# Modulation sums on GpSimd instead of VectorE and TensorE, and a lower load rate in the feed forward

## The chip, the cores and the metric

The program runs on one core of a Trainium2 chip. The metric is device time in microseconds from one launch, as the median of several runs. The engines are called as the profile calls them: TensorE (PE), its weight load (PEld), VectorE (DVE), ScalarE (ACT), GpSimd (POOL) and SyncE (SP), which here only issues loads.

## The reference

Two transformer-like blocks on a sequence of 256 tokens with 2048 features, in float32. In both, a conditioning vector `c` of 2048 numbers gives six modulation vectors of 2048 numbers each:

```python
c_act = jax.nn.silu(c)
mod = c_act @ w_ada[l] + b_ada[l]          # w_ada: 2048 x 12288
sh1, sc1, g1, sh2, sc2, g2 = split(mod, 6)
h = rms_norm(x, norm_mix_g) * (1.0 + sc1) + sh1
x = x + g1 * mixer(h)
h2 = rms_norm(x, norm_mlp_g) * (1.0 + sc2) + sh2
x = x + g2 * (square(relu(h2 @ w_ff1)) @ w_ff2)
```

The first block's mixer is a state-space branch and an attention branch with gates (`w_in`, `w_glu`, `w_proj_ssm`, `w_proj_attn`, `w_out`); its feed forward has 8192 hidden features. The second block has another mixer (`w_in_2`, `w_out_2`) and, in place of the feed forward, a lookup of expert rows by index (`peer_down`, `peer_up`). The twelve modulation vectors are read here by the pair (block, number): (1, 1) and (1, 0) are the first block's `sc1` and `sh1`, (2, 5) is the last gate of the second block.

## The kernel before

**Weight gemms.** A weight matrix is read in pieces of four k-chunks by 512 columns, 1 MB each (`piece`). A piece is split by ScalarE into a rounded half (`wh`, 1.9 us) and by VectorE into the rest (`wl`, a two-operand subtraction over 128x2048), and TensorE multiplies both by the two halves of the activations (`gemm`, tiles `ga` and `gb`). A piece costs 48 matmuls of 256 columns or 24 of 512. The halves have two buffers each (tags "H" and "L").

**Modulation vectors.** One vector is a product of `c_act` with 16 tiles of 128x2048 of the modulation weights, 1 MB each (`aw`). There are two ways: `ada_pe` lets TensorE multiply each tile by a replicated column of `c_act` (tile `adap`); `ada` calls `ada_acc`, where VectorE multiplies each tile by a column and adds it into a sum over partitions (`acc`, or `gB` for the vector (2, 5)), and at the end TensorE sums over the partitions with one set of four matmuls (`ada`), followed by a copy and transposes (`ada_fin`, tile `adat`). The vectors (1, 1) and (1, 0) are always made by `ada_pe`, ahead of everything else. The string `TUNE["pe"]` names the numbers of the first block's further vectors that go by `ada_pe`: "24" before, so (1, 2) and (1, 4).

**What sets the order.** Both kinds of loads are issued by SyncE and take their buffers from one ring of four (pool `wp`, tag "W"). The vectors wait in one list, `stream`. Inside `gemm`, after every group of matmuls, `bg` adds a credit, and for each whole credit one step of the first vector in the list is taken, that is one `aw` tile. The credit per piece is `rate`: `TUNE["r1"]`, 0.65 up to `w_out`; `TUNE["r2"]` in the feed forward, 0.84 before; 0.5 in `w_in_2`. The number that a step yields is VectorE time, counted against the credit for other VectorE work (`work`: state-space steps, attention heads). `need` takes all the steps that are left of the vectors it names, at once; it stands ahead of `w_out`, in the feed forward after its second block, and ahead of the feed forward's last gemm, where the five vectors (2, 1), (2, 0), (2, 2), (2, 4) and (2, 3) must be there:

```python
        while cred[1] >= 1.0 and stream:
            cred[1] -= 1.0
            cred[0] -= step(stream, False)
...
            if end:
                need((2, 1), (2, 0), *[(2, s_[1]) for s_ in later[:TUNE["nf"]]])
```

In most of the program a scheduler then arranges the instructions of each engine; in a few stretches (`pinned`) the order is that of the code. GpSimd's instructions are never pinned except the late gathers. GpSimd issues small loads at the start, then nothing, and from about 2000 us the gathers of expert rows (`gather`, tiles `dn` and `up`), whose dot products VectorE makes (`dn` with `htok`, a two-operand instruction).

Of the kernel before, what the change touches and what calls it, by code (L numbers as in the profile page):

```python
# [15 lines left out]
OP = mybir.AluOpType  # L16
# [15 lines left out]
def _consts():  # L32
# [29 lines left out]
    for j in range(512):  # L62
# [9 lines left out]

NU = 14

TUNE = {"r1": 0.65, "d1": 3.6, "pe": "24", "r2": 0.84, "d2": 3.0, "rg": 0.5, "dq": 5.2, "dk": 4.0, "dr": 2.6, "dx": 3.9,
        "do": 5.0, "ro": 0.0, "nf": 3, "tail": 2}


# [1 line left out]
def tile_kernel(ctx: ExitStack, tc: tile.TileContext, I, out):  # L80
# [20 lines left out]
    V, S, T = Pinned(nc.vector), Pinned(nc.scalar), Pinned(nc.tensor)  # L101
    G, SY = nc.gpsimd, nc.sync
    uid = [0]

    def nm(s):
        uid[0] += 1
        return f"{s}_{uid[0]}"
# [8 lines left out]
    dr = ctx.enter_context(tc.tile_pool(name="dr", bufs=1, space=DRAM))  # L116
# [4 lines left out]
    def unit(shape, name="u", dt=F32):  # L121
        return up.tile(shape, dt, name=nm(name), tag="U")
# [9 lines left out]
    def pacc_(shape, name="a"):  # L132
        return psa.tile(shape, F32, name=nm(name), tag="A")

    def pmisc(shape, name="m"):
        return psb.tile(shape, F32, name=nm(name), tag="B")
# [69 lines left out]
    def start(g, first=False):  # L206
        if first:
            work.insert(0, g)
        else:
            work.append(g)  # L210
        return g
# [5 lines left out]
    ccol = {1: cT[:, 0:16], 2: cT[:, 16:32]}  # L217
    mods = {}

    def ada_acc(blk, j, acc):  # L220
        w = adaw[blk]
        for kc in range(NC):
            wt = wp.tile([P, D], F32, name=nm("aw"), tag="W")
            SY.dma_start(wt, w[kc * P:(kc + 1) * P, j * D:(j + 1) * D])
            if kc == 0:
                V.tensor_scalar(acc, wt, ccol[blk][:, 0:1], None, op0=OP.mult)
            else:
                V.scalar_tensor_tensor(acc, wt, ccol[blk][:, kc:kc + 1], acc, op0=OP.mult, op1=OP.add)
            yield 2.2

    def ada_fin(blk, j, ps, dest, g):
        ev = scr([P, 512], "adae")
# [12 lines left out]
    def ada(blk, j, g=None):  # L245

        dest = const([P, 16], "mod")
        acc = unit([P, D], "acc")
        yield from ada_acc(blk, j, acc)
        ps = pmisc([P, 512], "ada")  # L250
        for q in range(4):
            T.matmul(ps[32 * q:32 * q + 32, :], ones[:, 0:32], acc[:, 512 * q:512 * q + 512],
                     start=True, stop=True, skip_group_check=True)
        ada_fin(blk, j, ps, dest, g)
        yield 0.2
# [77 lines left out]
    def rsqrt_of(ps, scale, w, r1=None):  # L333

        al = tiny if w <= 32 else scr
        v = al([P, w], "rv")
        if r1 is not None:
            V.tensor_mul(v, r1, r1)
            V.tensor_mul(v, v, ps)
            ps = v  # L340
        V.tensor_scalar(v, ps, scale, EPS, op0=OP.mult, op1=OP.add)
        r = al([P, w], "rr")
        S.activation(r, v, AF.Sqrt)
        V.reciprocal(r, r)
        t = al([P, w], "rt")
        V.tensor_mul(t, v, r)
        V.scalar_tensor_tensor(t, t, -0.5, r, op0=OP.mult, op1=OP.mult)
        V.scalar_tensor_tensor(r, t, 1.5, r, op0=OP.add, op1=OP.mult)
        return r
# [121 lines left out]
    def total(st):  # L471
        r = tiny([P, 2], "tot")
        V.tensor_reduce(r, st, axis=AX.X, op=OP.add)
        return r
# [448 lines left out]
    def queue_ada(*specs, pe=False):  # L923
        def run():
            for b_, j_, *g_ in specs:
                g_ = g_[0] if g_ else None
                yield from (ada_pe(b_, j_, g_, crep) if pe else ada(b_, j_, g_))
        stream.append(run())
# [6 lines left out]
    for j, g_ in ((2, None), (4, "norm_mlp_g"), (3, None), (5, None)):  # L935
        queue_ada((1, j, g_), pe=str(j) in TUNE["pe"])

    def store_pairs(dst, base, func=AF.Copy, scale=1.0):
        def ev(i, b):
            c = base + 2 * i  # L940
            S.activation(dst[c // 8][:, c % 8:c % 8 + 2, :], b, func, scale=scale)
        return ev

    uT = unit([P, 8, L], "uT")
    for nb in range(2):
        gemm(w_in, NC, nb * 512, [("A", 512, store_pairs([uT], 4 * nb))], h, rate=TUNE["r1"], dve=TUNE["d1"], pre=pre if nb == 0 else ())

# [48 lines left out]
    def moba(h0, h1):  # L996
        for hd in range(h0, h1, 2):
            pts = yield from attn_probs([(qT[:, hd + j, :], kT[:, hd + j, :]) for j in range(2)],
                                        [bias[:, hd + j, :] for j in range(2)])
            o = pmisc([P, 2, L], "o")  # L1000
            for j in range(2):
                hs = slice((hd + j) * P, (hd + j + 1) * P)
                attn_pv(o[:, j, :], pts[j], vt[:, 0, hs], vt[:, 1, hs], True, True)
            V.tensor_copy(qT[:, hd:hd + 2, :], o)
            yield 0.7
# [4 lines left out]
    for nb in range(2):  # L1010
        gemm(w_in, NC, 1024 + nb * 512, [("A", 512, store_pairs([qT], 4 * nb, scale=SCALE))], h, rate=TUNE["r1"], dve=TUNE["d1"])
    for nb in range(2):
        gemm(w_in, NC, 2048 + nb * 512, [("A", 512, store_pairs([kT], 4 * nb))], h, rate=TUNE["r1"], dve=TUNE["d1"])
    vt = unit([P, 2, 1024], "vt")
    g_moba = []
    for nb in range(2):
        def ev_v(i, b, nb=nb):
            S.copy(vt[:, i, nb * 512:nb * 512 + 512], b)
        gemm(w_in, NC, 3072 + nb * 512, [("B", 512, ev_v)], h, rate=TUNE["r1"], dve=TUNE["d1"])
        g_moba.append(start(moba(4 * nb, 4 * nb + 4), first=True))  # L1020

    sgb = [unit([P, 8, L], "sgb") for _ in range(2)]
    for nb in range(4):
        gemm(w_in, NC, 6144 + nb * 512, [("A", 512, store_pairs(sgb, 4 * nb, AF.Tanh, 0.5))], h, rate=TUNE["r1"], dve=TUNE["d1"])
        if nb == 2:
# [130 lines left out]
    r2 = rsqrt_of(total(sq2), 1.0 / D, 2, r1c)  # L1156
# [18 lines left out]
    def gt2_bcast():  # L1175
        acc = unit([P, D], "gB")
        yield from ada_acc(2, 5, acc)
        br = wp.tile([1, D], F32, name=nm("gb"), tag="W")
        SY.dma_start(br, I["ada_b_2"][:, 5 * D:6 * D])
        for q in range(4):  # L1180
            sl = slice(512 * q, 512 * q + 512)
            ps = pmisc([P, 512], "gbp")
            T.matmul(ps, ones, acc[:, sl], start=True, stop=False)
            T.matmul(ps, ones[0:1, :], br[:, sl], start=False, stop=True)
            S.copy(acc[:, sl], ps)
            yield 0.0
        mods["gB"] = acc
# [551 lines left out]
    for i in range(16):  # L1739
        qt, hd, ei, g, dots = items[i]  # L1740
        if hd == 0:
            acc = [pacc_([P, 512], "pe") for _ in range(3)] + [pmisc([P, 512], "pe")]
# [80 lines left out]
```

## Time and profile before

| | |
|---|---|
| median of 3 runs | 3320.3 us (3318.84 to 3320.39) |
| the profiled execution's own time | 3320.44 us |
| its span, first to last instruction | 3318.7 us, 39085 instructions |
| mean granted TensorE clock | 0.975 of 2.4 GHz |
| TensorE busy | 2966.0 us (89%) |
| VectorE busy | 2268.4 us (68%) |
| ScalarE busy | 951.7 us (29%) |
| GpSimd busy | 817.5 us (25%) |

Stages, by the first and last matmuls on their activations: the two first vectors and the normed input up to 114 us; projections, attention, state space and `w_out` from there to 806 us; feed forward to 1550 us; `w_in_2` from 1560 to 1853 us; then `w_out_2` and the expert rows to the end. Busy times of engines overlap; the share over the whole span is a mean of stages with different limits, so what one stage is bound by is read from that stage.

### The profile page before, as it was taken

How to read it: one execution, taken by the hardware profiler on the slowest of the kernel's cores; microseconds unless marked ns; L12 is line 12 of the kernel's file. 1: busy time of each engine (PE TensorE's matmuls, PEld its weight loads, DVE VectorE, ACT ScalarE, POOL GpSimd, SP SyncE). 2: the span in 40 equal slices, each digit the busy share in tenths (PEclk: the TensorE clock that was granted, in tenths of full speed). 3: DMA queues.
4: the chain of work that ended last, by engine and by line, in shares of the span. 5: the costliest groups of instructions: out<-in, count | busy, mean ns of one | idle time of the engine just before them, and what ended most of it. 6: DMA issues, size and time to landing. Idle time of an engine off the chain costs nothing.

```text
span 3318.7 us, 39085 instructions
## 1 busy us (share of the span) xinstructions
PE 2966.0 (89%) x15580; PEld 2151.7 (65%) x15580; DVE 2268.4 (68%) x3360; ACT 951.7 (29%) x1271; POOL 817.5 (25%) x540
## 2 busy tenths in 40 slices
PE   6899999999999999999999998988877768777777
PEld 2687889998998889997999886444322223222222
DVE  7687689877788888877766647545655565555642
ACT  1323433444443343345336731111111101111000
POOL 1000000000000000000000005556666666666663
PEclk8899999999999999999999998999999989999999
DMA  9866667877899999984883448999999999999998
GB/s 367 303 224 212 208 228 239 300 273 241 285 328 336 328 335 328 328 288 155 280 273 115 153 165 358 419 418 420 421 422 421 422 422 421 422 421 421 422 421 340
DMA packets 280459, 1068.90 MB, mean 322 GB/s; under 512 B 27380, under 2 KB 35991, under 8 KB 189525
## 3 DMA queue, kind: packets, MB, share of 16 engines
q1 hardware_dynamic: 202306, 524.35, 45.8%
q0 software_dynamic: 74752, 538.26, 39.1%
q10 hardware_dynamic: 3220, 3.81, 0.4%
q8 instruction: 122, 2.00, 0.2%
q14 instruction: 59, 0.48, 0.0%
HBM read 1064.24 MB, written 2.11 MB: 321 GB/s over the span
## 4 chain that ended last, share of the span: by engine, by line
PE 61%; DMA 29%; DVE 5%; issue 2%; POOL 1%; ACT 1%; SPq 0%; POOLq 0%; ACTq 0%; DVEq 0%
PE ga L94 31%; DMA dn<-in_peer_down_dram,eid 24%; PE gb L94 18%; PE pe L94 4%; DMA up<-in_peer_up_dram,eid 3%; DVE dn L94 2%; PE adap L94 2%; DMA aw<-in_w_ada_dram 2%; PE xt L94 1%; PE bu L94 1%; PE yp L94 1%; PE wqp L94 1%; PE o L94 1%; DMA up<-in_peer_up_dram,er 1%; POOL dn L1689 1%
## 5 line engine op out<-in xcount | busy, mean ns | idle before, releaser
L94 PE MATMUL pe<-up,cdg 128*128 128x512 f32 x1792 | 831.7, 613 | 258.9 <-DMA up<-in_peer_up_dram,eid 189.4
L1689 POOL DMA_INDIRECT dn<-in_peer_down_dram,eid x256 | 499.4, 1951 | 2256.4 <-DVE g L94 1969.3
L94 DVE SCALAR_TENSOR_TENSOR dn<-dn,htok 128x2048 f32<-128x2048 f32 x256 | 586.0, 2291 | 482.5 <-DMA dn<-in_peer_down_dram,eid 482.4
L94 PEld LDWEIGHTS pe<-up,cdg 128*128 128x128 f32 x1792 | 336.5, 195 | 744.0 <-issue 510.7
L94 ACT ACTIVATE wh<-w 128x2048 fp32r<-128x2048 f32 (+1 forms) x284 | 538.9, 1897 | 876.3 <-PE ga L94 488.5
L94 DVE TENSOR_TENSOR wl<-w,wh 128x2048 fp32r<-128x2048 f32 (+1 forms) x284 | 643.1, 2265 | 193.0 <-ACT wh L94 144.2
L1689 POOL DMA_INDIRECT up<-in_peer_up_dram,eid x224 | 266.5, 1190 | 155.6 <-issue 51.5
L94 DVE SCALAR_TENSOR_TENSOR acc<-aw,cT,acc 128x2048 f32<-128x2048 f32 x105 | 246.6, 2348 | 48.1 <-DMA aw<-in_ada_w_dram 29.9
L94 PE MATMUL ga<-h2h,wh 128*128 128x256 f32 x1024 | 249.1, 283 | 0.0
L94 PE MATMUL ga<-h2l,wh 128*128 128x256 f32 x1024 | 248.6, 283 | 0.0
L94 PE MATMUL ga<-h1h,wh 128*128 128x256 f32 x896 | 224.1, 289 | 0.0
L94 PE MATMUL ga<-h1l,wh 128*128 128x256 f32 x896 | 220.4, 284 | 0.0
L94 PE MATMUL gb<-wh,ah 128*128 128x512 f32 x512 | 199.6, 390 | 0.0
L94 PE MATMUL gb<-wh,al 128*128 128x512 f32 x512 | 199.4, 390 | 0.0
L94 PEld LDWEIGHTS ga<-h2h,wh 128*128 128x128 f32 x1024 | 196.5, 192 | 1.9 <-issue 1.7
L94 PEld LDWEIGHTS ga<-h2l,wh 128*128 128x128 f32 x1024 | 196.5, 192 | 0.2
L94 PEld LDWEIGHTS ga<-h1h,wh 128*128 128x128 f32 x896 | 172.7, 193 | 19.5 <-issue 15.3
L94 ACT ACTIVATE cdg<-ca,cf 128x128 f32<-128x128 f32 x224 | 77.0, 393 | 356.4 <-PE pe L94 345.9
L94 PEld LDWEIGHTS ga<-h1l,wh 128*128 128x128 f32 x896 | 172.9, 193 | 0.9 <-issue 0.8
L94 PE MATMUL ga<-h2h,wl 128*128 128x256 f32 x1024 | 134.1, 283 | 0.0
L94 PE MATMUL ga<-h3l,wh 128*128 128x256 f32 x528 | 132.1, 288 | 0.0
L94 PE MATMUL ga<-h3h,wh 128*128 128x256 f32 x528 | 132.0, 288 | 0.0
(444 smaller groups left out, 4327.4 us busy)
## 6 DMA issues: line engine op xcount, KB each, us to landing
w<-in_w_ff_dram SPq DMA_DIRECT2D x128, 1024.0 KB, 6.6
w<-in_w_in_dram SPq DMA_DIRECT2D x100, 1024.0 KB, 5.6
aw<-in_w_ada_dram SPq DMA_DIRECT2D x96, 1024.0 KB, 7.2
aw<-in_ada_w_dram SPq DMA_DIRECT2D x96, 1024.0 KB, 6.3
w<-in_w_out_dram SPq DMA_DIRECT2D x32, 1024.0 KB, 5.1
wq<-in_peer_wq_dram SPq DMA_DIRECT2D x16, 1024.0 KB, 10.2
w<-in_w_proj_attn_dram SPq DMA_DIRECT2D x8, 1024.0 KB, 5.0
w<-in_w_proj_ssm_dram SPq DMA_DIRECT2D x8, 1024.0 KB, 5.7
```

The source lines that it names most:

```text
L94: r = f(*a, **k)
L1689: r = G.indirect_dma_start(out=rows_, out_offset=None, in_=table, in_offset=bass.IndirectOffsetOnAxis(ap=idx, axis=0))
```

## The change

All vectors that were made by VectorE, and the two that TensorE made besides the first two, now go through `ada_acc`, and `ada_acc` issues on GpSimd. GpSimd has two instructions in place of VectorE's one: a multiply in place, then an add into the sum. The steps no longer count VectorE time, and the feed forward's rate of tiles per piece is 0.66.

```diff
-TUNE = {"r1": 0.65, "d1": 3.6, "pe": "24", "r2": 0.84, "d2": 3.0, ...
+TUNE = {"r1": 0.65, "d1": 3.6, "pe": "", "r2": 0.66, "d2": 3.0, ...
...
             if kc == 0:
-                V.tensor_scalar(acc, wt, ccol[blk][:, 0:1], None, op0=OP.mult)
+                G.tensor_scalar(acc, wt, ccol[blk][:, 0:1], None, op0=OP.mult)
             else:
-                V.scalar_tensor_tensor(acc, wt, ccol[blk][:, kc:kc + 1], acc, op0=OP.mult, op1=OP.add)
-            yield 2.2
+                G.tensor_scalar(wt, wt, ccol[blk][:, kc:kc + 1], None, op0=OP.mult)
+                G.tensor_add(acc, acc, wt)
+            yield 0.0
```

The change moves instructions on every engine. GpSimd, beside the first projections: before, the gathers of expert rows (`dn`) stand directly behind the two small copies of the attention bias.

```order
28 L855 DMA rdr<-rrs_343 8x512
29 L858 DMA rev_346<-rdr 128x8x256
30 L1689 DMA dn_18006<-in_peer_down_dram,eid_17995 128x2048
31 L1689 DMA dn_18011<-in_peer_down_dram,eid_17995 128x2048
32 L1689 DMA dn_18016<-in_peer_down_dram,eid_17995 128x2048
```

Now the tiles of vector (1, 2) stand there (the number is the tile's):

```order
28 L856 DMA rdr<-rrs_343 8x512
29 L859 DMA rev_346<-rdr 128x8x256
30 L226 ISA
31 L226 TENSOR_SCALAR acc_1123<-aw_1124,cT_94 128x2048
32 L228 TENSOR_SCALAR aw_1211<-aw_1211,cT_94 128x2048
33 L228 TENSOR_SCALAR aw_1297<-aw_1297,cT_94 128x2048
34 L229 TENSOR_TENSOR acc_1123<-acc_1123,aw_1211 128x2048
35 L229 TENSOR_TENSOR acc_1123<-acc_1123,aw_1297 128x2048
36 L228 TENSOR_SCALAR aw_1385<-aw_1385,cT_94 128x2048
37 L228 TENSOR_SCALAR aw_1467<-aw_1467,cT_94 128x2048
38 L229 TENSOR_TENSOR acc_1123<-acc_1123,aw_1385 128x2048
39 L228 TENSOR_SCALAR aw_1596<-aw_1596,cT_94 128x2048
```

310 such rows stand ahead of the first gather, and nearly everywhere the multiply of a tile (1467, 1596) stands ahead of the add of the tile before it.

SyncE, at the end of the feed forward: before, weight pieces of the feed forward alone stand ahead of the first two of the next block's `w_in`; the last `aw` tile is 23 pieces back, at row 391.

```order
411 L520 DMA w_13727<-in_w_ff_dram 128x4x512
412 L520 DMA w_13757<-in_w_ff_dram 128x4x512
413 L520 DMA w_13804<-in_w_ff_dram 128x4x512
414 L520 DMA w_13834<-in_w_ff_dram 128x4x512
415 L520 DMA w_13864<-in_w_in_dram 128x4x512
416 L520 DMA w_13947<-in_w_in_dram 128x4x512
```

Now, with `aw` tiles of vector (2, 3), taken up to `aw_13759` by the rate and then by `need`:

```order
398 L224 DMA aw_13691<-in_ada_w_dram 128x2048
399 L521 DMA w_13715<-in_w_ff_dram 128x4x512
400 L521 DMA w_13745<-in_w_ff_dram 128x4x512
401 L224 DMA aw_13759<-in_ada_w_dram 128x2048
402 L224 DMA aw_13793<-in_ada_w_dram 128x2048
...
412 L224 DMA aw_13833<-in_ada_w_dram 128x2048
413 L521 DMA w_13853<-in_w_ff_dram 128x4x512
414 L521 DMA w_13883<-in_w_ff_dram 128x4x512
415 L521 DMA w_13913<-in_w_in_dram 128x4x512
416 L521 DMA w_13996<-in_w_in_dram 128x4x512
```

Twelve tiles stand in a row, `aw_13759` and the 11 that `need` takes; the last gemm's two pieces and the next block's first two stand behind them. TensorE at the same place, in the last gemm (pieces 13853 and 13883, whose halves are `wh_13855`, `wh_13885`), now waits in its order for the sum of all 16 tiles:

```order
6643 L94 MATMUL gb_13851<-wh_13885,al_12765 128x512
6644 L94 MATMUL gb_13851<-wl_13886,ah_12764 128x512 x4
6645 L94 MATMUL ada_13837<-acc_13519,ones_87 32x512 x4
6646 L94 MATMUL adat_13844<-ca_81,adae_13842 128x128 x4
6647 L94 MATMUL gb_13852<-wh_13855,ah_12764 128x512
```

The last vector's matmul stands between the gemm's two halves, `gb_13851` and `gb_13852`.

## Rows read from the trace of the kernel before

**Rows 1.** Busy time of each engine in three stretches; PEclk is the granted clock.
```profile
114.00:806.00 692.00, 687.39 (x4869) 602.22 (x4869) 533.09 (x803) 262.92 (x264) 0.00 (x0) 1.00 0.73 245
806.00:1550.00 744.00, 741.27 (x4776) 673.21 (x4776) 611.31 (x439) 306.06 (x264) 0.00 (x0) 1.00 0.88 304
1560.00:1853.00 293.00, 293.00 (x2303) 280.13 (x2302) 218.76 (x391) 153.25 (x240) 0.00 (x0) 1.00 0.62 207
```

**Rows 2.** The same stretches, modulation tiles alone: PE, PEld, DVE busy, clock, DMA.
```profile
114.00:806.00 692.00, 35.50 (x248) 5.36 (x248) 58.88 (x26) 1.00 0.73 245
806.00:1550.00 744.00, 0.00 (x0) 0.00 (x0) 196.64 (x86) 1.00 0.88 304
1560.00:1853.00 293.00, 0.00 (x0) 0.00 (x0) 36.50 (x16) 1.00 0.62 207
```

**Rows 3.** SyncE's queue, its waits: 806 to 1550 us, then 114 to 806.
```profile
SPq L520 <- DVE wl L94: 212.4, 66, 6.9
SPq L520 <- DVE acc L94: 146.4, 62, 3.1
...
SPq L520 <- PE adap L94: 111.3, 17, 10.3
```

**Rows 4.** The chain that ended last, 1460 to 1560 us: start, length, what.
```profile
1463.04 0.99 PE ada L94 x8
...
1469.94 0.44 PE adat L94 x4
1470.38 76.00 PE gb L94 x335
```

**Rows 5.** Groups of VectorE instructions, 806 to 1550 us.
```profile
L94 DVE TENSOR_TENSOR wl<-w,wh 128x2048 fp32r<-128x2048 f32 x128 | 292.7, 2287 | 56.6 <-ACT wh L94 47.1 <-PE ga L94 5.7 <-issue 3.1
L94 DVE SCALAR_TENSOR_TENSOR acc<-aw,cT,acc 128x2048 f32<-128x2048 f32 x81 | 190.2, 2349 | 44.4 <-DMA aw<-in_ada_w_dram 29.9 <-DMA aw<-in_w_ada_dram 14.5
...
L94 DVE TENSOR_TENSOR x<-x,res 128x512 f32<-128x512 f32 x64 | 42.4, 687 | 0.5
L94 DVE TENSOR_TENSOR al<-relu,ah 128x512 fp32r<-128x512 f32 x32 | 21.7, 686 | 2.2 <-ACT ah L94 1.8
L94 DVE TENSOR_TENSOR relu<-relu 128x512 f32<-128x512 f32 x32 | 20.6, 685 | 0.0
L94 DVE TENSOR_SCALAR acc<-aw,cT 128x2048 f32<-128x2048 f32 x5 | 6.4, 1281 | 0.9 <-DMA aw<-in_ada_w_dram 0.9
```

**Rows 6.** Groups of VectorE instructions, 1560 to 1962 us: the scan.
```profile
L94 DVE TENSOR_TENSOR_SCAN hs<-lq,ig 128x256 f32<-128x256 f32 x8 | 5.0, 674 | 1.8 <-PE ga L94 1.8
```

**Rows 7.** DMA issues on the page: KB each, median us to landing.
```profile
w<-in_w_in_dram SPq DMA_DIRECT2D x100, 1024.0 KB, 5.6
...
aw<-in_ada_w_dram SPq DMA_DIRECT2D x96, 1024.0 KB, 6.3
```

**Rows 8.** Timeline from 2200 to 2213 us, GpSimd and then VectorE: start, length.
```profile
2201.22 2.43 POOL L1689 DMA_INDIRECT up<-in_peer_up_dram,eid  x1 [2.31 <-PE pe L94]
2204.46 0.94 POOL L1689 DMA_INDIRECT dn<-in_peer_down_dram,eid  x1 [0.81 <-DMA up<-in_peer_up_dram,eid]
2207.20 2.44 POOL L1689 DMA_INDIRECT up<-in_peer_up_dram,eid  x1 [1.80 <-DMA dn<-in_peer_down_dram,eid]
...
2212.43 0.94 POOL L1689 DMA_INDIRECT dn<-in_peer_down_dram,eid  x1 [0.30 <-issue]
...
2200.55 2.29 DVE L94 SCALAR_TENSOR_TENSOR dn<-dn,htok 128x2048 f32<-128x2048 f32 x1 [7.36 <-DMA dn<-in_peer_down_dram,eid]
...
2206.53 2.29 DVE L94 SCALAR_TENSOR_TENSOR dn<-dn,htok 128x2048 f32<-128x2048 f32 x1 [3.69 <-DMA dn<-in_peer_down_dram,eid]
```

**Rows 9.** The gathers' index tile: GpSimd's instruction, ns min, median and max.
```profile
L1689 POOL DMA_INDIRECT dn<-in_peer_down_dram,eid x256: 936/2365/3012, 2003.2 to 3246.6; - x128
```

**Rows 10.** Groups of VectorE instructions, 114 to 806 us, with a PSUM operand.
```profile
L94 DVE TENSOR_TENSOR sa<-bu,tab 128x512 f32<-128x512 f32 x32 | 21.9, 684 | 1.4 <-PE bu L94 1.4
...
L94 DVE TENSOR_TENSOR wr<-bu,tab 128x512 f32<-128x512 f32 x16 | 11.0, 688 | 31.4 <-PE bu L94 31.4
...
L94 DVE TENSOR_TENSOR wi<-bu,tab 128x512 f32<-128x512 f32 x16 | 10.9, 681 | 0.0
```

More of the change, by code (lines that the diff above doesn't have):

```diff
@@ L73 @@
 NU = 14
-TUNE = {"r1": 0.65, "d1": 3.6, "pe": "24", "r2": 0.84, "d2": 3.0, "rg": 0.5, "dq": 5.2, "dk": 4.0, "dr": 2.6, "dx": 3.9,
+TUNE = {"r1": 0.65, "d1": 3.6, "pe": "", "r2": 0.66, "d2": 3.0, "rg": 0.5, "dq": 5.2, "dk": 4.0, "dr": 2.6, "dx": 3.9,
         "do": 5.0, "ro": 0.0, "nf": 3, "tail": 2}
```

## The prediction

> **What bounds the kernel now.** I read the stretches first. From 114 to 806 us (the first projections up to `w_out`) and from 806 to 1550 us (the feed forward) TensorE is busy for 687.39 of 692 us and 741.27 of 744 us at the full granted clock [rows 1]. So in these stretches TensorE is the bound; VectorE, with 533.09 and 611.31 us, has slack. From 1560 to 1853 us TensorE is busy throughout as well. After 1853 us no modulation tile is left, and the change moves nothing there. The modulation tiles in these windows cost TensorE 35.50 us, all before 806 us, and VectorE 58.88, 196.64 and 36.50 us [rows 2].
>
> Then I looked at what SyncE's queue waits for. All loads of weight pieces (`w`, L520) and modulation tiles (`aw`) stand in one queue and take turns in one ring of four buffers. In the feed forward a piece's load stands for 212.4 us in all until VectorE has split an older piece, and for 146.4 us until VectorE has added an older modulation tile; before 806 us it stands for 111.3 us behind TensorE's own modulation matmuls [rows 3]. None of this reaches TensorE today, but it says who will decide when a piece arrives: whoever reads the tile that holds the buffer.
>
> **The change, part by part.**
>
> *TensorE's two vectors.* 35.50 us of matmuls leave a stretch in which TensorE is the bound [rows 2]. Each vector gets back one set of four matmuls on the sum; 8 rows of the like lasted 0.99 us [rows 4], so two sets are 2. Gain: 33 us, as long as nothing else becomes the bound.
>
> *VectorE's 128 tiles.* 292.02 us of VectorE work go [rows 2]. Where TensorE is the bound they are worth nothing: they lay beside the matmuls.
>
> *GpSimd's tiles.* 160 tiles, each now two instructions over 128x2048: a multiply by a scalar in place, then an add into the sum. No row shows GpSimd doing such work, so I bound the two together, c. Below: as quick as VectorE in these shapes, 1.28 for the multiply and 2.29 for the two-input instruction [rows 5], 3.6 us. Above: the slowest rate per element of an elementwise pass that I find, VectorE's scan, 674 ns for 256 columns [rows 6], so 5.4 us for 2048 and 10.8 us for two passes. The middle of these is 7.2, their geometric mean 6.2; nothing in the trace is nearer, and I take 6.7 us.
> The Trainium skill, page "GPSIMD Engine Reference", section "Performance versus the Vector engine", gives 4497 ns for the two-input add of 2048 floats and about one cycle per element at 1.2 GHz for one input: an estimate of 6.3 us by that page. By it the sum below would come to 3715 us. No run here shows either price yet.
>
> *The ring.* This is the main cost. GpSimd's order, shown with the change, is: multiply tile n+1, then add tile n. So the buffer of tile n is not free when tile n is done, but only when tile n+1 has landed, been multiplied, and tile n has then been added. The load four places behind tile n takes that buffer. With about two tiles in five loads, it stands behind tile n+1 and ahead of tile n+2 (or is n+2). So from the issue of n+1 to that of n+2 pass at least: landing + c. Landing has a median of 6.3 us for the second block's tiles; the DMA engines will be less pressed than now, so I take the 5.6 us that the pieces of `w_in` have [rows 7]. The period is 5.6 + 6.7 = 12.3 us. In the feed forward 77 tiles stand in turn with the pieces (8 left of vector (1,5) and 80 of five vectors, less the run of 11 below); 744 us leave 9.7 us for each. The ring is therefore slower than TensorE there.
>
> *VectorE and GpSimd together.* Does one hold up the other? The gathers show it. GpSimd's gather instruction takes 0.94 us when VectorE is between its long instructions (2204.46, 2212.43). The one at 2201.22 lasts 2.43 us and ends at 2203.65, 0.81 us after VectorE's `dn` instruction (2200.55 to 2202.84); the one at 2207.20 ends at 2209.64, 0.82 us after the next (2206.53 to 2208.82) [rows 8]. Over all 256 `dn` gathers the minimum is 0.936 us and the median 2.365 [rows 9]. So a GpSimd instruction that meets a VectorE instruction with two operands in SBUF waits for its end.
> The Trainium skill, page "SBUF — State Buffer", section "Who interferes with whom", says this as a rule: VectorE with two SBUF inputs and GpSimd reading SBUF exclude each other for the whole instruction. By that rule, the trace agrees in the direction that it can show; that a long GpSimd instruction holds up VectorE no row shows. The rule speaks against this change, since both new instructions read SBUF.
> The cost: in the feed forward VectorE keeps 292.7 + 42.4 + 21.7 + 20.6 = 377 us of two-input SBUF work [rows 5], 4.9 us per tile. A share of 4.9/12.3 = 0.4 of GpSimd's instructions finds one in progress, with half of 2.29 us to go: 0.4 x 1.15 x 2 = 0.9 us per tile. The period becomes 13.2 us, and 77 x 13.2 = 1016 us: **+272** against 744.
> Ahead of 806 us, VectorE's 533.09 less 58.88 less the 43.8 us of the three largest groups that read one operand from PSUM [rows 10] leaves 430 us; smaller such groups are not taken off. With 56 tiles, three vectors and half of the fourth, exclusion makes 430 + 56 x 6.7 = 805 us, more than the ring's 56 x 13.2 = 739. I take 805: **+113** against 692; TensorE's 33 us are lost in it.
> From 1560 us: 16 tiles x 13.2 = 211 us, and by exclusion 16 x 6.7 plus VectorE's 218.76 - 36.50, 289 us, both under 293: nothing, and if that cover is gone, some 10 us.
>
> *The lower rate.* At 0.66 instead of 0.84 tiles per piece the five vectors of the second block are not through when the last weight gemm asks for them. The order shows 11 tiles in one run on SyncE ahead of the feed forward's last two pieces, and TensorE's matmul on the last sum between the halves of the last gemm. When TensorE starts on the piece ahead of that, it has two pieces of 24 matmuls; 335 such in 76.00 us [rows 4] make 5.4 us for a piece. GpSimd then has 12 tiles to do, alone: 12c. After the sum that matmul and its transposes, some 2 us, and half the gemm, 5.4 us, follow, where now four pieces, 21.8 us, would end. Loss: 12c - 14 = **66 us**. Queued behind the run are also the first two pieces of the next block's `w_in`, which wait at the same buffers.
>
> *Work that is only reordered.* The helper that paces VectorE's side work no longer counts 2.2 us per tile, so state-space steps stand elsewhere in VectorE's order. It is the same work beside the same matmuls: nothing.
>
> **The sum.** 113 + 272 + 66 = 451 us. The profiled execution took 3320.4 us, the median of the runs 3320.3, so they need no correction: 3771, say **3770 us**.
>
> **The rivals.**
> *No exclusion between long elementwise instructions* (the gather's wait would be one of descriptor writing only). The ring remains: 77 x 12.3 = 947, +203; ahead of 806 us 56 x 12.3 = 689, as now; the run 66. 3320 + 269 = 3589 us. For it: VectorE's `dn` instructions keep 2.29 us beside gathers. Against: the 0.81 us after VectorE's end. Chance 0.20.
> *GpSimd is far slower*, c = 10.8: ring 17.3 x 77 = 1332, +588; 430 + 605 = 1035, +343; run 116: 4367 us. Chance 0.10 for more than 4050.
> *GpSimd is cheap, c = 3.6*: ring 10.1 x 77 = 778, +34; 430 + 202 = 632, under TensorE's 659, so -33; run 29: 3350 us. Chance 0.04.
> *Faster.* With c at VectorE's single pass, 2.35 us [rows 5], the ring's 8.9 us per tile is under 9.7 and hidden, TensorE's 33 us are real, and the run costs 12 x 2.35 - 14 = 14: 3301 us. It decides from c below about 3.2 us, where the period meets 9.7; the run alone eats the gain at 3.9. For it: TensorE is the bound now. Against: two passes in place of one. Chance 0.03; no measurable change, within 0.2%, which is what a measurement of this kernel can tell: 0.02.
> *Forecast*: 0.61, with its own range 3600 to 4000 from c between 5.5 and 8.2. The range 3450 to 4050 takes in the rival without exclusion and leaves out less than 2 in 10. Slower: 0.95.
>
> **What would show it.** The two GpSimd rows: means that add up to about 6.7 us alone, seen in the run of 11 where VectorE is idle. In the feed forward SyncE's waits for GpSimd's add replace those for VectorE's; tiles are issued some 13 us apart; TensorE waits for ScalarE's and VectorE's halves of pieces, 744 us become about 1016. VectorE's two-input instructions beside GpSimd's are longer, or start late, if exclusion goes both ways. One gap of about 60 us on TensorE near the end of the feed forward. Before 806 us about 805 us. It is wrong if TensorE stays full there, if the tiles' period is under 10 us, or if GpSimd's pair takes under 4 us.

## The result, and the profile after

The changed kernel takes 4167.7 us (median of four runs, 4160.88 to 4169.61) against 3320.35: 1.2551 times as long, 95% interval 1.2533 to 1.2568. The prediction said 3770 us, 3450 to 4050: the sign was right, the size was not. The profiled execution took 4160.88 us, span 4159.1.

By the first matmuls on each stage's activations (`h2h` for the feed forward, `h3h` for `w_in_2`), in us. "The run" is the row of 12 tiles at the feed forward's end; the feed forward ahead of it, where the rate sets tiles between pieces, is called paced:

| stage | before | after | difference | predicted |
|---|---|---|---|---|
| up to the feed forward | 814.4 | 1098.7 | +284 | +113 |
| feed forward, without the run at its end | 748.1 | 1129.3 | +381 | +272 |
| TensorE's one long wait at that run | 0 | 109.0 | +109 | +66 |
| `w_in_2`, first to last matmul | 288.8 | 358.0 | +69 | 0 |
| the rest | 1467.4 | 1464.1 | -3 | 0 |

Four stretches of the kernel after, by busy time (PE, PEld, DVE, ACT, POOL; then granted clock, DMA share, GB/s); the first, second and fourth answer to [rows 1]:

```profile
114.00:1090.00 976.00, 736.88 (x4638) 655.68 (x4638) 780.62 (x777) 262.76 (x265) 634.99 (x110) 0.86 0.50 172
1090.00:2190.00 1100.00, 840.29 (x4716) 736.80 (x4714) 718.44 (x343) 298.89 (x250) 843.08 (x147) 0.88 0.55 192
2190.00:2323.00 133.00, 17.95 (x60) 11.79 (x60) 20.85 (x11) 9.30 (x13) 117.75 (x24) 0.55 0.37 122
2323.00:2650.00 327.00, 276.35 (x2061) 265.93 (x2062) 251.73 (x331) 120.50 (x186) 174.39 (x31) 0.90 0.52 173
```

In none of these stretches is TensorE the bound any longer. The line to stop at is VectorE's: in the feed forward it lost the 196.64 us of modulation tiles [rows 2] and is busy for 718 us in place of 611. Without the tiles it would be 611.3 - 196.6 = 415, so 303 us have been added to instructions that nobody changed. Its groups in the feed forward show which; `wl` and `x` answer to [rows 5] (busy, mean ns of one, idle before):

```profile
L94 DVE TENSOR_TENSOR wl<-w,wh 128x2048 fp32r<-128x2048 f32 x125 | 455.7, 3656 | 282.3 <-ACT wh L94 280.9 <-PE adat L94 1.4
L94 DVE TENSOR_TENSOR x<-x,res 128x512 f32<-128x512 f32 x62 | 102.1, 1651 | 1.3
...
L94 DVE TENSOR_TENSOR res<-gb,grow 128x512 f32<-128x512 f32 x62 | 42.2, 685 | 62.0 <-PE gb L94 62.0
```

The split went from a mean of 2287 to 3656 ns and `x` from 687 to 1651, while `res`, which reads one operand from PSUM, stayed at 685. Its row before:

```profile
L94 DVE TENSOR_TENSOR res<-gb,grow 128x512 f32<-128x512 f32 x64 | 42.7, 686 | 22.7 <-PE gb L94 21.8 <-issue 0.9
```

Ahead of the feed forward the same division runs through most of VectorE's groups, and short instructions are not spared: `sa` has a PSUM operand [rows 10], and `zin`, one column wide, has a mean of 144 ns before and 708 after. Its row before:

```profile
L94 DVE TENSOR_TENSOR zin<-wr,el 128x1 f32<-128x1 f32 x32 | 4.4, 144 | 0.0
```

Rows of the same stage after:

```profile
L94 DVE TENSOR_TENSOR wl<-w,wh 128x2048 fp32r<-128x2048 f32 x101 | 325.5, 3228 | 161.4 <-ACT wh L94 156.0 <-ACT grow L94 2.8 <-PE ga L94 2.5
...
L94 DVE TENSOR_TENSOR_SCAN wi<-prm,wi 128x128 f32<-128x128 f32 x32 | 31.3, 1019 | 0.0
...
L94 DVE TENSOR_TENSOR zin<-wr,el 128x1 f32<-128x1 f32 x32 | 22.5, 708 | 0.0
L94 DVE TENSOR_TENSOR sa<-bu,tab 128x512 f32<-128x512 f32 x32 | 21.7, 679 | 0.3 <-PE bu L94 0.3
```

The mean hides the form. Most `zin` rows last as long as before, and a few wait out a GpSimd instruction (shortest, median and longest, in ns):

```profile
L94 DVE TENSOR_TENSOR zin<-wr,el x32: 127/145/4525, 182.6 to 753.9; 128x1 f32<-128x1 f32 x32
```

Not every instruction with operands in SBUF alone is hit: the scan `wi<-prm,zin,wi` keeps its mean (468 ns before, 465 after). Why, no run settles.

GpSimd's price stands where VectorE has nothing to do, in the run of tiles at the feed forward's end (GpSimd's timeline):

```profile
2227.53 5.43 POOL L228 TENSOR_SCALAR aw<-aw,cT 128x2048 f32<-128x2048 f32 x1
2232.94 4.49 POOL L229 TENSOR_TENSOR acc<-acc,aw 128x2048 f32<-128x2048 f32 x1
2237.41 5.43 POOL L228 TENSOR_SCALAR aw<-aw,cT 128x2048 f32<-128x2048 f32 x1
2242.83 4.49 POOL L229 TENSOR_TENSOR acc<-acc,aw 128x2048 f32<-128x2048 f32 x1
```

So c, the pair for one tile, is 5.43 + 4.49 = 9.92 us; the prediction took 6.7 between bounds of 3.6 and 10.8. In the paced feed forward the means are longer still, 6.68 and 4.90:

```profile
L228 POOL TENSOR_SCALAR aw<-aw,cT 128x2048 f32<-128x2048 f32 x71 | 474.0, 6676 | 231.5 <-DMA aw<-in_ada_w_dram 160.9 <-issue 41.6 <-DMA aw<-in_w_ada_dram 12.5
L229 POOL TENSOR_TENSOR acc<-acc,aw 128x2048 f32<-128x2048 f32 x71 | 347.6, 4896 | 0.7
```

TensorE's timeline at the same run of tiles, with the one long wait that was foreseen:

```profile
2183.27 1.98 PE L94 MATMUL gb<-wl,ah 128*128 128x512 f32 x8
2294.20 0.79 PE L94 MATMUL gb<-wh,ah 128*128 128x512 f32 x1 [108.96 <-ACT wh L94]
```

SyncE's waits in the feed forward, which answer to [rows 3], are not what the prediction named. It expected waits for GpSimd's add; they are for VectorE's splits, which had been 212.4 us:

```profile
SPq L521 <- DVE wl L94: 437.6, 78, 25.6
SPq L224 <- DVE wl L94: 255.8, 45, 11.1
...
SPq L521 <- POOL acc L229: 28.6, 7, 4.1
```

TensorE's waits there are for both halves of late pieces, ScalarE's more than VectorE's; before, it had none of them:

```profile
PE gb L94 <- ACT wh L94: 112.4, 31, 5.2
PE ga L94 <- ACT wh L94: 87.2, 25, 6.0
PE ga L94 <- DVE wl L94: 30.2, 13, 4.7
PE gb L94 <- DVE wl L94: 21.6, 10, 5.6
```

### The profile page after: what moved, and what is told of

The parts are those of the page before. It is cut to its first block, busy times and chain, and to the rows that moved or that the text cites. A ratio compares the mean times of both kernels' runs of the same rounds, so it can differ in the third digit from the quotient of the medians.

```text
span 4159.1 us, 38797 instructions
## 1 busy us (share of the span) xinstructions
PE 3147.2 (76%) x15340; PEld 2296.2 (55%) x15340; DVE 2700.9 (65%) x3232; ACT 952.0 (23%) x1270; POOL 2594.7 (62%) x850
## 4 chain that ended last, share of the span: by engine, by line
DMA 36%; DVE 28%; PE 15%; issue 11%; ACT 5%; POOL 4%; SPq 0%; ACTq 0%; POOLq 0%; DVEq 0%
DMA dn<-in_peer_down_dram,eid 19%; DVE wl L94 12%; DMA w<-in_w_ff_dram 8%; PE ga L94 6%; ACT wh L94 5%; PE gb L94 4%; DMA up<-in_peer_up_dram,eid 3%; DVE p L94 3%; DMA w<-in_w_in_dram 2%; PE pe L94 2%; POOL aw L228 2%; DVE wr L94 2%; POOL acc L229 2%; DVE wi L94 1%; DMA aw<-in_w_ada_dram 1%
## 5 line engine op out<-in xcount | busy, mean ns | idle before, releaser
L228 POOL TENSOR_SCALAR aw<-aw,cT 128x2048 f32<-128x2048 f32 x150 | 957.1, 6381 | 653.4 <-DMA aw<-in_ada_w_dram 250.1
L94 DVE TENSOR_TENSOR wl<-w,wh 128x2048 fp32r<-128x2048 f32 (+1 forms) x284 | 930.2, 3282 | 598.6 <-ACT wh L94 583.9
L229 POOL TENSOR_TENSOR acc<-acc,aw 128x2048 f32<-128x2048 f32 x135 | 677.3, 5017 | 1.7
L94 PE MATMUL gb<-wh,ah 128*128 128x512 f32 x512 | 234.4, 458 | 226.5 <-ACT wh L94 226.5
L94 PE MATMUL ga<-h2h,wh 128*128 128x256 f32 x1024 | 279.4, 307 | 87.2 <-ACT wh L94 87.2
L94 PE MATMUL ga<-h2l,wh 128*128 128x256 f32 x1024 | 274.5, 303 | 1.1 <-DVE h2l L94 1.1
L94 PEld LDWEIGHTS ga<-h2h,wh 128*128 128x128 f32 x1024 | 218.4, 213 | 95.0 <-ACT wh L94 94.0
L94 PEld LDWEIGHTS gb<-wh,ah 128*128 128x128 f32 x512 | 114.6, 224 | 265.9 <-ACT wh L94 240.2
L94 PE MATMUL gb<-wh,al 128*128 128x512 f32 x512 | 227.9, 445 | 0.0
L94 PE MATMUL ga<-h1h,wl 128*128 128x256 f32 x896 | 129.7, 299 | 45.8 <-DVE wl L94 45.8
```

Of the source, the lines that this page charges most:

```text
L94: r = f(*a, **k)
L228: G.tensor_scalar(wt, wt, ccol[blk][:, kc:kc + 1], None, op0=OP.mult)
L229: G.tensor_add(acc, acc, wt)
```

## Experiments

The variants of the changed kernel (`gp_`) and the program of pairs have one execution each; the four of the changed kernel itself lie within 8.7 us. All differences by stage are between profiled executions.

**The engines by themselves.** A program of sections; the two calls of a pair are issued in turn on their own engines, with no dependence between them:

```python
G.tensor_scalar(gb, gb, cg[:, 0:1], None, op0=OP.mult)   # 6 times
V.tensor_sub(vo, va, vb)                                  # 16 times, beside it
```

> A program of its own (none of the reference's computation): sections in which GpSimd, VectorE and ScalarE repeat one instruction over 128x2048 alone and then two engines at once. Theory (one port, held for a whole instruction): six GpSimd multiplies (5.43 us each in the kernel after the change) beside 16 VectorE subtractions of two SBUF operands (2.29 us each) end after about the sum, 32.6 + 36.6 = 69 us, and single VectorE rows grow to as much as 7.7 us; six GpSimd adds (4.49) beside 14 of them, 27 + 32 = 59 us. With one VectorE operand in PSUM, and beside ScalarE, the longer of the two alone (about 33 us) stays. Rival (the two share a bandwidth, or the longer rows of the changed kernel come from its waits for semaphores): no section with two SBUF operands lasts longer than 1.3 times its longer half, and rows stretch evenly instead of ending just behind a GpSimd row. Alone, multiply and add should show 5.43 and 4.49 us, the shortest rows of the changed kernel.

From the timeline: the sections of one engine alone, and then pairs (start, length of the whole section, engine):

```profile
24.12 33.09 POOL L87 TENSOR_SCALAR gb<-gb,cg 128x2048 f32<-128x2048 f32 x6
...
58.13 27.37 POOL L87 TENSOR_TENSOR go<-ga,gb 128x2048 f32<-128x2048 f32 x6
...
201.02 13.94 DVE L87 TENSOR_TENSOR vo<-va,vb 128x2048 f32<-128x2048 f32 x6
...
262.15 57.47 DVE L87 TENSOR_TENSOR vo<-va,vb 128x2048 f32<-128x2048 f32 x16
264.47 36.13 POOL L87 TENSOR_SCALAR gb<-gb,cg 128x2048 f32<-128x2048 f32 x6
...
320.56 57.72 DVE L87 TENSOR_TENSOR vo<-va,vb 128x2048 f32<-128x2048 f32 x14
322.85 36.99 POOL L87 TENSOR_TENSOR go<-ga,gb 128x2048 f32<-128x2048 f32 x6
...
436.89 21.60 DVE L87 TENSOR_TENSOR vo<-va,ps 128x512 f32<-128x512 f32 x30
437.02 27.46 POOL L87 TENSOR_TENSOR go<-ga,gb 128x2048 f32<-128x2048 f32 x6
...
533.42 23.22 DVE L87 TENSOR_TENSOR vo<-va,vb 128x2048 f32<-128x2048 f32 x10
535.70 18.55 POOL L87 MEMSET gb<- 128x2048 f32 x10
```

Six adds beside 14 subtractions end after 57.7 us; the sum of both alone would be 27.4 + 14 x 2.32 = 59.9, the longer alone 32.5. That is exclusion, in both directions: nearly all the time only one of the two works. With one operand in PSUM neither engine notices the other (21.60 and 27.46 us, as alone), nor with a GpSimd memset, which only writes (1.85 us each). The multiply came out softer than the theory: 57.5 us where the sum is 70. The single rows of that section say why (shortest, median and longest, in ns):

```profile
L87 POOL TENSOR_SCALAR gb<-gb,cg x6: 5624/5625/7537, 264.5 to 295.0; 128x2048 f32<-128x2048 f32 x6
```

```profile
L87 DVE TENSOR_TENSOR vo<-va,vb x9: 2282/5682/5685, 262.1 to 301.0; 128x2048 f32<-128x2048 f32 x9
```

The two engines take turns, one multiply and one subtraction in 5.7 us, not in 5.43 + 2.29 = 7.7: a multiply keeps a subtraction out for some 3.4 us, not for all of its time. For an add the turn is 6.42 us, 0.36 less than 4.49 + 2.29.

**Shorter GpSimd instructions.**

```diff
-                G.tensor_scalar(wt, wt, ccol[blk][:, kc:kc + 1], None, op0=OP.mult)
-                G.tensor_add(acc, acc, wt)
+                for q in range(4):
+                    s_ = slice(512 * q, 512 * q + 512)
+                    G.tensor_scalar(wt[:, s_], wt[:, s_], ccol[blk][:, kc:kc + 1], None, op0=OP.mult)
+                for q in range(4):
+                    s_ = slice(512 * q, 512 * q + 512)
+                    G.tensor_add(acc[:, s_], acc[:, s_], wt[:, s_])
```

> The changed kernel with each GpSimd multiply and add cut into four of 128x512. Theory (GpSimd and VectorE's two-operand instructions exclude each other and their sum fills the time): the sum stays, so the time stays within 4% above 4168 us (up to 4330 with the start-up of more instructions). Rival (not the sum but the single long wait hurts: a weight split that finds a 4.5 or 5.4 us GpSimd instruction in progress): the mean split in the feed forward falls from 3.66 towards 2.5 us, about 140 us less there and about 100 less ahead of it: about 3930 us.

4089 us, between the two: less than the theory allows, and far from the rival's 3930. Up to the feed forward 1027.2 us (71 less than after the change) and 318 for `w_in_2` (40 less), but 1280 for the feed forward (42 more, with 125 in place of 109 for the run). VectorE is relieved in every stage, and the split's mean in the feed forward falls from 3656 to 2632 ns, as the rival had it. GpSimd pays: it is busy for 1078 us there in place of 843. The likely reason, not shown row by row, is that each of its eight instructions may now wait for a whole subtraction. So shorter turns help ahead of the feed forward, where VectorE has long rows of short instructions; in the feed forward they only move the wait to GpSimd.

**No lag between multiply and add.**

```diff
...
-                G.tensor_scalar(wt, wt, ccol[blk][:, kc:kc + 1], None, op0=OP.mult)
-                G.tensor_add(acc, acc, wt)
+                tc.keep_in_program_order(G.tensor_scalar(wt, wt, ccol[blk][:, kc:kc + 1], None, op0=OP.mult))
+                tc.keep_in_program_order(G.tensor_add(acc, acc, wt))
```

> The changed kernel with GpSimd's instructions held in the order of the code: multiply tile n, add tile n, then tile n+1. Theory (the shared port's sum is the bound): within 2.5% of 4168 us. Rival (the ring, as the prediction had it: a tile's buffer comes free only after the next tile has landed and been multiplied): the lag is gone, a tile's period in the feed forward falls from 14.5 us to about 10 (multiply and add, 9.92), and the kernel to about 3820 us.

4120.5 us, 1.1% less, as the theory had it. The lag, on which the prediction's ring period rests, is worth 36 us in the feed forward (1202.0 against 1238.3), 14 of them at the run; the rival had some 350.

**Five buffers.**

```diff
-NU = 14
+NU = 13
...
-    wp = ctx.enter_context(tc.tile_pool(name="wp", bufs=4))
+    wp = ctx.enter_context(tc.tile_pool(name="wp", bufs=5))
...
```

> The changed kernel with a ring of five buffers for weight pieces and modulation tiles in place of four (and one unit buffer less, 13 for 14). If the period of 14.5 us per tile in the feed forward is set by how long four buffers are held (loads waiting for late splits and late adds), five carry a quarter more loads: 14.5 falls to about 11.6, 76 x 2.9 = 220 us less there and some 50 to 100 less before and after: about 3870 us. Rival (the shared port is full): within 2% of 4168 us. In between tells the share of each.

4143 us, 0.6% less, as the rival had it; the feed forward 1235.7 against 1238.3. The number of buffers is not what bounds the feed forward.

**GpSimd as slow, but not reading.**

```diff
-                G.tensor_scalar(wt, wt, ccol[blk][:, kc:kc + 1], None, op0=OP.mult)
-                G.tensor_add(acc, acc, wt)
+                for _ in range(5):
+                    G.memset(wt, 0.0)
```

> The changed kernel with the multiply and the add of the tiles 1 to 15 of a vector replaced by five memsets of the tile's buffer on GpSimd (1.85 us each alone, 9.3 together against 9.9): it leaves the modulation sums out. GpSimd waits for the same landings, holds the same buffers of the ring for as long and is as slow, but reads nothing from SBUF. Theory (what costs is the port that GpSimd and VectorE's two-operand instructions share): TensorE is the bound again but for the run of 12 tiles ahead of the last gemm, 12 x 9.3 - 14 = 97 us; 3320 - 33 + 97 = 3384, up to 3450 with some waits at the ring. Rival (the ring of four buffers and GpSimd's slowness, landing + c for each tile): as the kernel in GpSimd's program order, which has no lag either, about 4120 less 0.6 us for each of 150 tiles: 3950 to 4120 us.

3470 us: 20 us above the theory's range, and 480 below the rival's. This settles most of it: the same loads, the same ring, GpSimd nearly as long in each buffer (9.3 us for 9.9), and 691 us of span less than the changed kernel (3468.2 against 4159.1). Two other things went with the reads: the lag between multiply and add, alone worth 40 us of span (4118.7 in gp_order), and 0.6 us of each tile, at most 0.6 x 160 = 96 us. So 550 us or more are left for what GpSimd reads. The feed forward of this run ahead of the 12 tiles, and the split there:

```profile
789.00:1570.00 781.00, 746.05 (x4722) 670.10 (x4721) 431.66 (x344) 299.30 (x255) 662.70 (x363) 0.98 0.78 272
```

```profile
L94 DVE TENSOR_TENSOR wl<-w,wh 128x2048 fp32r<-128x2048 f32 x125 | 296.0, 2368 | 269.3 <-ACT wh L94 260.2 <-PE ga L94 6.9 <-PE gb L94 2.0
```

GpSimd is busy for 663 of 781 us and VectorE's split is back at 2.37 us, near 2.29. What is left over the kernel before, 150 us, is the run (89.6 us of TensorE's wait), 53 in the paced feed forward, 30 in `w_in_2`, less 17 ahead of it and 5 at the end: this much is a slow GpSimd holding buffers without that lag.

**The multiply alone.**

```diff
                 G.tensor_scalar(wt, wt, ccol[blk][:, kc:kc + 1], None, op0=OP.mult)
-                G.tensor_add(acc, acc, wt)
```

> The changed kernel without the add on GpSimd: the multiply of a tile stays, in place, and the sum holds the first tile alone (it leaves the modulation sums out). If GpSimd's instruction counts with its whole duration against VectorE's two-operand work: 76 x 5.43 + 372 = 785 us in the paced feed forward (+41), 430 + 54 x 5.43 = 723 before it (+31), the run 12 x 5.43 - 14 = +51, 0 to 30 behind: 3443 to 3475 us. If only the part that holds the shared port counts, 3.4 us as the pairs showed, both sums are below TensorE's own time, and the run is left: 3320 - 17 + 51 = 3354, up to 3385 us.

3416.5 us, between the two ranges. The run's wait is 33.0 us. Up to the feed forward it is 27.7 us longer than before, near the 31 of the whole duration; but there TensorE waits 20.5 us for state-space products, which a VectorE with a little more work also brings about (below), so this part doesn't decide. The feed forward without the wait takes 799.5 - 33.0 = 766 against 748: +18 against +41 or nothing. `w_in_2` takes 22 us more than before (310.8). How long a multiply counts stays undecided; that adding the add to this kernel costs 750 us is shown.

**The rate.**

```diff
-TUNE = {"r1": 0.65, "d1": 3.6, "pe": "", "r2": 0.66, ...
+TUNE = {"r1": 0.65, "d1": 3.6, "pe": "", "r2": 0.84, ...
```

> The changed kernel with the feed forward's rate back at 0.84 tiles per piece: the run of 12 tiles ahead of the last gemm is gone, and its tiles stand between the pieces before. Theory (the port's sum, with the holds that the pairs showed, 3.4 us for a multiply beside a two-operand subtraction and 4.2 for an add): the paced part costs 88 x 7.6 + 334 of VectorE's two-operand work = 1003 us and the 13 pieces behind it 75, 1078 against 1233 now: about 4010 us. Rival 1 (each tile costs a fixed period, 14.5 us as now, whatever stands between): 88 x 14.5 + 75 = 1351, about 4285 us. Rival 2 (the run is a loss by itself, as the prediction had it, 12c - 14 = 105 us, and the rest stays): 4060 us.

4249 us, near rival 1. The theory, a sum with the holds of the pairs, is 240 us too low, and rival 2 is 190 too low. The long wait is gone, and the feed forward takes 1342.7 us in place of 1238.3. In the paced part a tile costs its 14 to 15 us here too; the lower rate saved the changed kernel 81 us. Some 54 of them are 12 tiles done alone at 9.9 in place of 14.4; the rest was not traced.

The lower rate alone, on the kernel before:

```diff
-TUNE = {"r1": 0.65, "d1": 3.6, "pe": "24", "r2": 0.84, ...
+TUNE = {"r1": 0.65, "d1": 3.6, "pe": "24", "r2": 0.66, ...
```

> The kernel before with the feed forward's rate at 0.66 alone: 12 tiles stand in a run ahead of the last two pieces, done by VectorE at 2.35 us each or as fast as they land (1 MB at the 389 GB/s of the last stage: 2.7 us). By the prediction's formula with c = 2.7: 12 x 2.7 - 14 = 18 us slower, 3338 us. Rival (the run is hidden, since the four buffers fill while TensorE works): within 5 us of 3320.

3360.35 us, ratio 1.0123 (1.0108 to 1.0138): 40 us, above both expectations. The feed forward accounts for 26 of them (774.5 against 748.1; TensorE's longest wait 23.1 us), where the formula has 18. The cause of some 5 us ahead of it and 8 behind it stays open.

**The other part: TensorE's two vectors, on VectorE.** The string `"24"` becomes empty in the kernel before (ve_all); only one of its two numbers goes (`"2"` in ve_pe2, `"4"` in ve_pe4); it becomes empty and a step counts 0.0 (ve_y0, shown here).

```diff
-TUNE = {"r1": 0.65, "d1": 3.6, "pe": "24", "r2": 0.84, ...
+TUNE = {"r1": 0.65, "d1": 3.6, "pe": "", "r2": 0.84, ...
...
                 V.scalar_tensor_tensor(acc, wt, ccol[blk][:, kc:kc + 1], acc, op0=OP.mult, op1=OP.add)
-            yield 2.2
+            yield 0.0
```

> The kernel before with TensorE's two vectors accumulated as well, but on VectorE (its fused instruction, 2.35 us a tile), and the rate 0.84 kept: one part of the change without GpSimd. If the prediction's term (a) is right, TensorE loses 35.5 us of matmuls ahead of 806 us and gains 2 back: 3287 us, 1.0% faster. Rival: VectorE, with 533 + 32 x 2.35 = 608 us of work in what would be 659 us, is late for weight splits, and 5 to 33 us of the gain go: 3290 to 3320.

> The kernel before with the vector (1, 4) alone moved from TensorE to VectorE, (1, 2) left on TensorE. Theory (VectorE's state-space products are what TensorE waits for once VectorE has both vectors, 44.7 us with a step counted as 2.2): half the tiles, half of TensorE's gain, 17 us, and none or little of the wait: 3303 to 3315 us. Rival (any tile more makes the state space late): 3325 to 3340 us.

> The kernel before with the vector (1, 2) alone moved from TensorE to VectorE, (1, 4) left on TensorE; (1, 2) is made first, while the state space is under way. Theory: as with (1, 4), 3303 to 3315 us if the wait for state-space products stays small; since its tiles stand earlier, ahead of the products, the rival, 3325 to 3340 us, is likelier here than there.

> All of the change's first part on VectorE: TensorE's two vectors accumulated by VectorE, and a step counts 0.0 instead of 2.2 us against the credit for other VectorE work, as in the change. In the run with 2.2 TensorE waited 44.7 us for the state-space products p. Theory (that wait comes from the credit: more tiles count 2.2 each, so state-space steps stand later): the wait goes and TensorE's 33 us show: 3285 to 3300 us. Rival (VectorE is simply full, 603 us of work in the stage): the wait turns up at the weight splits instead, 3320 to 3345 us.

| | us | ratio, interval |
|---|---|---|
| both on VectorE, 2.2 counted (ve_all) | 3342.2 | 1.0067, 1.0054 to 1.0081 |
| (1, 4) alone (ve_pe2) | 3333.7 | 1.0040, 1.0026 to 1.0054 |
| (1, 2) alone (ve_pe4) | 3330.2 | 1.0030, 1.0019 to 1.0042 |
| both, 0.0 counted (ve_y0) | 3326.8 | 1.0020, 1.0011 to 1.0029 |

All four miss the time that their theories gave. Three lie where their rivals had them (`ve_pe2`, `ve_pe4`, `ve_y0`), `ve_all` above both; `ve_y0`'s rival had looked for the wait at the splits. TensorE waits in the same place in each, for products of the state space (tile `yp`): 44.7, 24.3, 18.3 and 18.7 us in the order of the table, and not at all before. The stretch in which the state space ends, 614 to 664 us, in `ve_all` and in `ve_y0`:

```profile
614.00:664.00 50.00, 14.21 (x47) 6.87 (x48) 47.57 (x123) 0.00 (x0) 0.00 (x0) 0.56 0.09 34
```

```profile
614.00:664.00 50.00, 26.60 (x170) 20.55 (x169) 38.75 (x70) 12.12 (x16) 0.00 (x0) 0.73 0.32 116
```

TensorE has 14 and 27 us of work in 50, VectorE 48 and 39. VectorE had slack as a mean over the stage, 533 of 692 us busy, but not enough ahead of this point: from 114 to 614 us it was busy for 388 of 500 us before, and is for 436 and 453 in these two.

**A version faster than both.** As ve_y0, with fewer tiles before that point (rates 0.56 and 0.90 in ve_r56, 0.50 and 0.95 in ve_r50, shown here):

```diff
-TUNE = {"r1": 0.65, "d1": 3.6, "pe": "24", "r2": 0.84, ...
+TUNE = {"r1": 0.5, "d1": 3.6, "pe": "", "r2": 0.95, ...
...
-            yield 2.2
+            yield 0.0
```

> A try at a version faster than both: all vectors but the first two on VectorE, a step counted as 0.0, with fewer tiles ahead of the feed forward (rate 0.56 for 0.65) and more in it (0.90 for 0.84), where VectorE has slack. In the run with 0.65 VectorE was 88 to 95% busy from 164 to 614 us and TensorE then idle for 23 us. 5 tiles fewer ahead of that, 12 us of VectorE's work, should take some 12 us off that idle time: 3310 to 3318 us. Rival (the state space's steps depend on more than VectorE's free time): 3322 to 3332 us.

> The same with rates 0.50 and 0.95: 10 tiles fewer ahead of the idle stretch, 23 us of VectorE's work, but five tiles in a run ahead of the last four pieces of the output gemm: 3300 to 3312 us if the run stays hidden, 3315 to 3330 if it doesn't.

With 0.56 and 0.90: 3315.0 us, 0.9986 (0.9977 to 0.9995). With 0.50 and 0.95: 3303.55 us, 0.9956 (0.9941 to 0.9972), 16.5 us faster than before. Both lie in their expected ranges. The same stretch with 0.50 and 0.95:

```profile
614.00:664.00 50.00, 45.32 (x347) 43.18 (x348) 35.39 (x34) 22.51 (x24) 0.00 (x0) 0.90 0.62 225
```

Its feed forward begins at 788.6 us, 25.8 earlier than before, and TensorE waits 2.8 us for `yp`. Most of TensorE's 33 us are real once VectorE isn't late.

## Why the prediction was wrong

Two steps failed, one in its size and one in its mechanism.

**The size: c, under "GpSimd's tiles".** It is 9.92 us, not 6.7: inside its bounds, but 3.2 us short for each of 160 tiles. This is why the forecast was too low. With 9.92 the prediction's own formulas give 985 us ahead of 806 (976 measured from 114 on) and 12 x 9.92 - 14 = 105 for the run (109 of wait): those mechanisms hold and only their size was off. The whole sum would be 3320 + 293 + 519 + 105 = 4237 us, above the 4168 measured; the 519 are the feed forward's, where 381 were measured. Alone the add takes 4.49 us and the multiply 5.43. The Trainium skill ("GPSIMD Engine Reference", "Performance versus the Vector engine") has 4497 ns for the add, and the trace agrees. The estimate of 6.3 from the same section had some 1.8 for the multiply; there the measurement decides.

**The mechanism: the feed forward, under "VectorE and GpSimd together".** There the prediction took a period set by the ring and added 0.9 us per tile, for GpSimd's wait alone. VectorE's wait was named among the signs to look for, but had no price in the sum. Measured per tile: GpSimd waits (843 - 71 x 9.92 - 5 x 5.43)/76 = 1.5 us, and VectorE 303/76 = 4.0. SyncE's 437.6 us show loads waiting for those splits. The memset run shows that this exclusion, and not the ring, is most of the loss: with the ring as it was, the paced feed forward took 801 us and not 1129. With c set right, the ring's formula would have been too long here (below), so the two errors partly cancelled in the forecast.

What the price of exclusion is, stays open in part. A sum of what the two engines do one after the other gives 71 x 9.92 + 5 x 5.43 + 372 of VectorE's two-operand work (125 splits at 2.29, 126 shorter ones at 0.69) = 1103 us against 1100 measured. The prediction used this kind of sum ahead of 806 us and thought the ring larger in the feed forward. That it fits to 3 us is partly luck: multiply and subtraction overlap by 2 us where they meet; in gp_multonly the same sum is 54 us too long (72 x 5.43 + 27 + 372 = 790 against 736), and in gp_r84 65 too short (83 x 9.92 + 27 + 335 = 1185 against 1250).

**The ring.** Overpriced. Its formula with c = 9.92 and the 0.9 gives 16.4 us per tile, 77 x 16.4 = 1263 us; measured are 14.5 per tile and 1129 us. The lag is worth 1.1% of the kernel, a fifth buffer 0.6%, and a GpSimd that holds buffers for 9.3 us without the lag costs 53 us in the paced part.

**Exclusion as such.** Right. The Trainium skill, "SBUF — State Buffer", "Who interferes with whom": by its rule VectorE with two SBUF inputs and GpSimd reading SBUF keep each other out, and a GpSimd instruction that only writes does not; the pairs agree with both halves (57.7 us against 59.9 and 32.5; 23.2 beside memsets). "For the whole instruction", as the prediction put it, nearly holds for the add, some 4.1 of 4.49 us; for the multiply the pairs show some 3.4 of 5.43.

**TensorE's 33 us.** The term was true as work and void as time: "as long as nothing else becomes the bound" was broken by VectorE's state-space steps when VectorE took the tiles, and by the exclusion when GpSimd did. "Work that is only reordered: nothing" was wrong in the same stretch: counting 0.0 for 2.2 alone moves ve_all by 15 us.

**From 1560 us.** Zero was predicted with a cover that was nearly used up, 289 of 293 us, and "some 10" without it; with c = 9.92 the exclusion sum there is 16 x 9.92 + 182 = 341, and 358 were measured. The gather rows of before pointed the right way on exclusion. The chance of 0.10 for a GpSimd this slow was too small for a cost that no row showed.

## What to carry to other kernels

Before work goes to an idle engine, ask what that engine shares with the one it relieves: here a tile that VectorE did itself took 2.3 us of its time (292.02/128), beside TensorE's matmuls, and a tile that GpSimd did cost it more, 4.0 us in the feed forward and (780.6 - 474.2)/56 = 5.5 ahead of it. A wait between engines is to be priced on both sides, and on every short instruction of the side that has many. A mean over a stage is no slack: whether an engine has room is read from the stretch ahead of the point where another waits for it, and a rate that moves work behind that point can turn a loss into a gain.

## What the runs showed of the hardware beyond that

GpSimd's one-input multiply by a column (5.43 us for 128x2048) is slower than its two-input add (4.49), and it makes no difference whether it is in place (six in 33.09 and 33.10 us). VectorE's one-input multiply over 128x2048, 1.28 us in the kernel before, also takes turns with it: 20 of them beside six multiplies last 56.7 us, and 14 beside ten memsets 33.7 (alone the six take 33.1 us, the ten 18.6), where the two-operand subtraction isn't touched by a memset. TensorE's granted clock fell where it idles between pieces: means of 0.86 and 0.88 in the two long stages of the changed kernel, against 1.00 before, and nearly the same matmuls are busy for 840 us in the feed forward in place of 741. Whether these 99 us lengthened the kernel, or only filled time in which TensorE would have waited, no run separates.
